# Gate rows transposed on VectorE before they are written, and the linear attention's output products grouped by tile shape

## The chip, the cores and the metric

One program on one core of a Trainium2 chip. Its engines run separate instruction streams and meet at semaphores: TensorE (PE in the profile; PEld is its weight load), VectorE (DVE), ScalarE (ACT), GpSimd (POOL) and SyncE (SP, which here only issues DMAs). Each engine works its stream off in order. Sixteen DMA engines move data between DRAM, the on-chip SBUF and back. The metric is the device time of one execution in microseconds; three executions of the kernel before took 1444.01, 1446.22 and 1446.49, the median is 1446.22.

## The reference: what is computed

Two layers of an encoder trunk over 512 tokens of width 1024, all in f32. A conditioning vector c gives six vectors of 1024 per layer: shift, scale and gate for each of two sub-layers.

```
for l in range(DEPTH):                                   # DEPTH = 2
    mod = silu(c) @ ada_w[l] + ada_b[l]
    sh1, sc1, g1, sh2, sc2, g2 = split(mod, 6)
    hn = rmsnorm(x, pre_mix_g[l]) * (1 + sc1) + sh1
    y = token_mixer(hn, ...)        # retention | stick-breaking | gated linear attention
    x = x + g1 * rmsnorm(y, post_mix_g[l])
    hn = rmsnorm(x, pre_ffn_g[l]) * (1 + sc2) + sh2
    y = conv_ffn(hn, ...)
    x = x + g2 * rmsnorm(y, post_ffn_g[l])
```

The gated linear attention (four heads of 64) works in eight chunks of 64 tokens. A chunk's output is the sum of an inner part, scores of the chunk times its values, and a carried part, the query times the state left by the chunks before:

```
inter = einsum('bhcd,bhde->bhce', q_i * exp(b_i), state)
intra = einsum('bhts,bhse->bhte', scores, v_i)
out_i = inter + intra
```

## The kernel before

Activations lie with the features on the 128 partitions and the 512 tokens along the free dimension, or, for the residual x and for what closes a sub-layer, with the tokens on the partitions in four blocks (`tb` 0 to 3) of 128. A weight product is made of three products of parts (`mm3`, L355): a weight tile `raw` comes by DMA on SP's queue, ScalarE rounds it into `hi` (L351) and VectorE leaves the rest in `lo` (L352). PE's stream is written out by hand-made orders (`TOK` at L55, `PQ` at L53) and a scheduler that keeps each engine's instructions in the order in which it chose them; nothing is reordered on the chip by data arriving late.

**The gates.** `ada_steps` (L238) computes half of one of a layer's six vectors: eight loads of a 128x512 piece of `ada_w` on SP's queue, each multiplied by c on VectorE and summed (L249), then the bias (L254, L255) and, for a gate, the norm's weight (L259). The result is `modT`, 128 partitions by 8 columns, where element (p, k) belongs to feature 128k + p. The calls are spread between other work by `fill`: gate 1 of layer 0 during the first mixer, gate 2 of layer 0 and gate 1 of layer 1 during the first feed-forward part, gate 2 of layer 1 at its very end, while the last products of that part run. A gate must multiply along the free dimension where tokens lie on the partitions (`close0` L503, `close1` L510), so it is turned into a row of 1024 in DRAM (`rows`, L262) and read back to all 128 partitions (`load_gate`, L266). Both DMAs are issued by GpSimd (`QUEUE` sends kind "row" to it). The write at L262 puts each of the 1024 elements to its place separately, as 4 bytes:

```
ld(rows[l, which].rearrange("o (k p) -> p (o k)", p=P), modT[l, which], False, "row")
```

GpSimd also computes every norm's power -1/2 (L285), in order with those DMAs.

**The end of a feed-forward part.** For each token block `close1` squares, multiplies by the gate, loads x (`load_x`, SP's queue), adds (L519), stores x and hands the tile to `prenorm`, whose transposes on PE with the scaled identity `dg` (L303, L321) give the next layer's input. Between them PE already runs the next layer's first projection (`proj_tok`, stick-breaking values, 24 products for a token block into one of three banks `pj`).

**The linear attention's output** (`gla_pair`, L741 to L758) is made for two heads together, in two PSUM banks `o`, one for even and one for odd chunks. For each chunk c in turn two products of 64x64 tiles add the inner part (scores `sc` times values `vtok`) and one product over all 128 rows with 64 columns adds the carried part (states `st` times decayed query `qd`), so tile shapes alternate chunk by chunk. This happens four times: two head pairs in each of two layers. The banks' marks are set anew by `start=True` in each chunk.

Of the kernel before, what the change touches and what calls it, by code (L numbers as in the profile page):

```python
# [11 lines left out]
F32 = mybir.dt.float32  # L12
# [7 lines left out]
P = 128  # L20
S = 512
D = 1024
KT = D // P
# [3 lines left out]
CH = 64  # L27
NCH = S // CH
# [69 lines left out]
def trunk(ctx: ExitStack, tc: tile.TileContext, A, out, dbg=None):  # L98
    nc = tc.nc

    cp = ctx.enter_context(tc.tile_pool(name="cp", bufs=1))
# [15 lines left out]
    def nm(s):  # L117
        cnt[0] += 1
        return f"{s}_{cnt[0]}"

    def T(tag="m", shape=(P, 512), dt=F32):
        tag = TMAP.get(tag, tag)
        return tiles[tag].tile(list(shape), dt, tag=tag, name=nm(tag + "_"))

    def small(n):
        return sp.tile([P, 8], F32, tag="s", name=nm("s"))[:, :n]
# [11 lines left out]
    def pso():  # L138
        return bank("po")
# [4 lines left out]
    V, SC, G, PE = nc.vector, nc.scalar, nc.gpsimd, Recorder(nc.tensor)  # L144

    @contextmanager
    def seq(kind):

        mode = MODE[kind]
        m = (None, PE.last, PE.lastp)[mode]  # L150
        if m is not None:
            with tc.issue_after(m.ins):
                yield
        else:
            yield
        if kind == "p":
            PE.lastp = PE.last

    lastw = [None]
    start = {"on": True, "ld": None, "pe": None, "ws": []}  # L160

    def ld(t, src, gated=False, kind=None):
        q = QUEUE.get(kind, "sp")
        if q != "sp":
            return (G if q == "g" else SC).dma_start(t, src)


        m = lastw[0] if gated else start["ld"]
        if m is None:
            r = nc.sync.dma_start(t, src)  # L170
        else:
            with tc.issue_after(m.ins):
                r = nc.sync.dma_start(t, src)
        if start["on"]:
            start["ld"] = r
        return r
# [57 lines left out]
    modT = {}  # L234
# [3 lines left out]
    def ada_steps(l, g):  # L238
        which, half = WHICH[g // 2], g % 2
        if half == 0:  # L240
            modT[l, which] = cp.tile([P, KT], F32, tag=f"mod{l}{which}", name=f"mod{l}{which}")
        pt = small(8)
        for j in range(4):
            for h in range(2):
                raw = ap_.tile([P, 512], F32, tag="ada", name=nm("ada"))
                r_ = ld(raw, A["ada"][l, g // 2, 4 * half + j, :, 512 * h : 512 * h + 512], False, "ada")
                if "ada" not in QUEUE:
                    lastw[0] = r_
                V.scalar_tensor_tensor(raw, raw, 1.0, cB[h], ALU.mult, ALU.mult, accum_out=pt[:, 4 * h + j : 4 * h + j + 1])  # L249
                if (2 * j + h) % FSTEP == FSTEP - 1:  # L250
                    yield
        m = modT[l, which][:, 4 * half : 4 * half + 4]
        o = PV[which] + 4 * half
        V.tensor_tensor(m, pt[:, 0:4], pt[:, 4:8], ALU.add)  # L254
        V.tensor_tensor(m, m, pv[l][:, o : o + 4], ALU.add)  # L255
        if which[0] == "g":

            o = PV["p" + which] + 4 * half
            V.tensor_tensor(m, m, pv[l][:, o : o + 4], ALU.mult)  # L259
            if half:  # L260
                rows[l, which] = dp.tile([1, D], F32, tag=f"{which}{l}", name=f"{which}row{l}")
                ld(rows[l, which].rearrange("o (k p) -> p (o k)", p=P), modT[l, which], False, "row")  # L262

    rows = {}

# [266 lines left out]
    def mixer(l, hnh, hnl, after):  # L532
# [115 lines left out]
        def gla_pair(j):  # L648
# [14 lines left out]
            sc = T("gl", (P, 2, NCH // 2, CH))  # L663
# [15 lines left out]
            for n in range(len(LEVELS) + 1):  # L679
# [3 lines left out]
                with seq("g"):  # L683
                    for c in range(NCH):
                        odd, cs = 64 * (c % 2), slice(c * CH, c * CH + CH)
# [12 lines left out]
                if n == len(LEVELS):  # L698
                    b3 = b.rearrange("p (c t) -> p c t", t=CH)
                    kd, qd = T("gl"), T("gl")  # L700
# [17 lines left out]
            st = [T("gl", (P, 4, P)) for _ in range(2)]  # L718
# [5 lines left out]
            with seq("g"):  # L724
                for c in range(NCH - 1):
                    rows = slice(64 * (c % 2), 64 * (c % 2) + 64)
                    PE.matmul(pk[c % 2][:, (c // 2) * P : (c // 2) * P + P], kdT[rows, c // 2, :],
                              vtok[c // 2][rows, j * P : j * P + P], start=True, stop=True)
            for c in range(NCH - 1):
                for h in range(2):  # L730
                    rows = slice(64 * h, 64 * h + 64)
# [8 lines left out]

            o = [pso(), (psz, psg)[GB > 0]()]  # L741
            with seq("g"):
                for c in range(NCH):
                    odd = slice(64 * (c % 2), 64 * (c % 2) + 64)
                    cs = slice(c // 2 * CH, c // 2 * CH + CH)
                    for h in range(2):
                        PE.matmul(o[c % 2][64 * h : 64 * h + 64, cs],
                                  vtok[c // 2][odd, j * P + 64 * h : j * P + 64 * h + 64],
                                  sc[odd, h, c // 2, :], start=True, stop=(c == 0), skip_group_check=True)
                    if c:  # L750
                        PE.matmul(o[c % 2][:, cs], st[(c - 1) // 4][:, (c - 1) % 4, :],
                                  qd[:, c * CH : c * CH + CH], start=False, stop=True, skip_group_check=True)
            go[j] = T("gl")
            g4 = go[j].rearrange("p (c o t) -> p c o t", o=2, t=CH)
            for odd in range(2):
# [117 lines left out]
        for u in range(4):  # L873
            wh, wl = unit(A["wo"][l, 0, u], (P, 2, 512))
            for kk in range(2):
                k = KPERM[2 * u + kk]
                for tb in range(NTB):
                    cs = slice(tb * P, tb * P + P)
# [3 lines left out]
        for tb in range(NTB):  # L882
            cs = slice(tb * P, tb * P + P)
            ps = psz()
            for i in range(KT):
                k = KPERM[i]
# [272 lines left out]
```

## Time and profile before

| | |
|---|---|
| median of three executions | 1446.22 us |
| the profiled execution's own time | 1440.25 us |
| its span, first to last instruction | 1438.5 us |
| PE busy | 1374.8 us, 96% of the span |
| DVE busy | 831.9 us, 58% |
| ACT busy | 674.5 us, 47% |
| POOL busy | 36.2 us, 3% |
| mean granted TensorE clock | 0.985 |
| DRAM read, written | 176.51 MB, 8.41 MB |

The profile is one execution; its rows give start and length of each instruction, the idle time before it and what ended that idle time. The profiled execution was 5.97 us shorter than the median of the unprofiled three. A share of busy time is a mean over unlike stages: the two mixers (60 to 345 and 757 to 1045 us in this trace), the two feed-forward parts, the start and the end; what an edit in one of them is worth is read there.

### The profile page before, as it was taken

The page shows a single profiled execution, that of the slowest core. Times are in us where ns is not written, and L with a number is a line of the kernel's source. Part 1 is how long each engine was busy: PE and PEld are TensorE (multiplying, and loading weights), DVE is VectorE, ACT ScalarE, POOL GpSimd, SP SyncE. Part 2 cuts the span into 40 slices and gives each one's busy share as a digit, 9 for nine tenths or more (in the row PEclk, how much of TensorE's full clock was granted, in tenths as well). Part 3 has the DMA queues.
Part 4 walks back from the last instruction along what each step waited for, and adds up shares of the span by engine and source line. Part 5 has one row for each costly group of instructions (what it writes and reads, how often), then busy time and mean ns, then how long its engine had stood idle before and what let it go on. Part 6 is the DMA issues. An engine that isn't in the chain of part 4 may idle for free.

```text
span 1438.5 us, 19727 instructions
## 1 busy us (share of the span) xinstructions
PE 1374.8 (96%) x7619; PEld 1123.4 (78%) x7619; DVE 831.9 (58%) x1544; ACT 674.5 (47%) x1105; POOL 36.2 (3%) x57
## 2 busy tenths in 40 slices
PE   8999789989999999999999999998999999999998
PEld 5887667768878778888879877776789888888886
DVE  4459887655878674432654487586665444443232
ACT  5565466755533233332244676766655333333130
POOL 0000000000000000000010000000010000000000
PEclk9999999999999999999999999999999999999999
DMA  8636461203688762222773221112152222222222
GB/s 312 215 127 151 157 204 51 74 16 134 225 246 264 199 228 95 103 88 103 249 162 127 88 89 59 45 59 74 45 205 101 90 103 90 101 101 90 103 103 103
DMA packets 73614, 186.22 MB, mean 129 GB/s; under 512 B 8448, under 2 KB 9520, under 8 KB 73520
## 3 DMA queue, kind: packets, MB, share of 16 engines
q1 hardware_dynamic: 72512, 182.68, 39.0%
q0 software_dynamic: 704, 2.11, 0.4%
q8 instruction: 60, 0.98, 0.3%
q14 instruction: 34, 0.28, 0.1%
q10 hardware_dynamic: 304, 0.16, 0.0%
HBM read 176.51 MB, written 8.41 MB: 129 GB/s over the span
## 4 chain that ended last, share of the span: by engine, by line
PE 54%; DMA 7%; DVE 7%; ACT 5%; issue 2%; POOL 0%; DVEq 0%; SPq 0%; POOLq 0%; ACTq 0%
PE pj L91 30%; PE ps L91 24%; DMA ada<-ada 6%; DVE lo L352 1%; DVE ada L249 1%; ACT hi L351 1%; DMA m__1230_6531<-x 0%; DMA m__707_3538<-x 0%; DMA raw<-wu 0%; DMA raw<-wT 0%; DVE hnl L332 0%; POOL s L285 0%; ACT m__1645_8747 L577 0%; ACT m__1407_7530 L577 0%; ACT m__1283_6827 L577 0%
## 5 line engine op out<-in xcount | busy, mean ns | idle before, releaser
L352 DVE TENSOR_TENSOR lo<-raw,hi 128x1024 fp32r<-128x1024 f32 (+2 forms) x208 | 245.7, 1184 | 263.3 <-ACT hi L351 258.0
L91 PE MATMUL pj<-hnh,hi 128*128 128x512 f32 x976 | 384.5, 394 | 7.2 <-DVE m__873_4577 L911 3.9
L91 PE MATMUL pj<-hnl,hi 128*128 128x512 f32 x976 | 383.6, 393 | 0.0
L91 PE MATMUL pj<-hnh,lo 128*128 128x512 f32 x976 | 382.7, 392 | 0.0
L351 ACT CAST hi<-raw 128x1024 fp32r<-128x1024 f32 (+2 forms) x208 | 211.1, 1017 | 336.4 <-PE pj L91 177.7
L91 PEld LDWEIGHTS pj<-hnh,hi 128*128 128x128 f32 x976 | 184.5, 189 | 47.6 <-issue 10.2
L91 PEld LDWEIGHTS pj<-hnl,hi 128*128 128x128 f32 x976 | 184.1, 189 | 37.7 <-issue 1.0
L91 PEld LDWEIGHTS pj<-hnh,lo 128*128 128x128 f32 x976 | 184.2, 189 | 37.5
L249 DVE SCALAR_TENSOR_TENSOR ada<-ada,cB 128x512 f32<-128x512 f32 x160 | 107.4, 689 | 45.1 <-DMA ada<-ada 44.5
L91 PE MATMUL pj<-hi,hnh 128*128 128x384 f32 (+1 forms) x160 | 52.8, 330 | 5.1 <-ACT m__1254_6623 L541 3.8
L91 PE MATMUL pj<-lo,hnh 128*128 128x384 f32 (+1 forms) x160 | 52.2, 326 | 0.4 <-DVE lo L352 0.4
L91 PE MATMUL pj<-hi,hnl 128*128 128x384 f32 (+1 forms) x160 | 52.1, 326 | 0.0
L285 POOL TENSOR_TENSOR s<-s,nhalf 128x1 f32<-128x1 f32 x32 | 20.3, 633 | 783.4 <-DVE s L283 779.3
L91 PE MATMUL ps<-hnl,hi 128*128 128x256 f32 x128 | 36.2, 287 | 1.3 <-DVE hnl L332 1.3
L91 PEld LDWEIGHTS pj<-hi,hnh 128*128 128x128 f32 x160 | 31.1, 194 | 6.1 <-ACT m__1254_6623 L541 4.0
L91 PE MATMUL ps<-hnh,lo 128*128 128x256 f32 x128 | 35.8, 283 | 0.0
L91 PE MATMUL ps<-hnh,hi 128*128 128x256 f32 x128 | 35.7, 289 | 0.0
L513 ACT ACTIVATE junk<-ps 128x512 bf16<-128x512 f32 x16 | 9.5, 596 | 52.3 <-PE ps L91 52.0
L91 PEld LDWEIGHTS pj<-lo,hnh 128*128 128x128 f32 x160 | 31.0, 194 | 1.0 <-DVE lo L352 0.7
L91 PEld LDWEIGHTS pj<-hi,hnl 128*128 128x128 f32 x160 | 30.9, 193 | 0.0
L91 PEld LDWEIGHTS ps<-hnl,hi 128*128 128x128 f32 x128 | 24.5, 193 | 1.7 <-DVE hnl L332 1.7
L91 PEld LDWEIGHTS ps<-hnh,hi 128*128 128x128 f32 x128 | 24.6, 197 | 0.0
(2794 smaller groups left out, 2523.5 us busy)
## 6 DMA issues: line engine op xcount, KB each, us to landing
raw<-wu SPq DMA_DIRECT2D x88, 512.0 KB, 3.3
ada<-ada SPq DMA_DIRECT2D x160, 256.0 KB, 3.7
raw<-wd SPq DMA_DIRECT2D x44, 512.0 KB, 3.2
raw<-wT SPq DMA_DIRECT2D x42, 512.0 KB, 3.5
raw<-wo SPq DMA_DIRECT2D x16, 512.0 KB, 3.2
raw<-wsv SPq DMA_DIRECT2D x8, 384.0 KB, 3.5
raw<-wrv SPq DMA_DIRECT2D x8, 384.0 KB, 3.0
raw<-wgv SPq DMA_DIRECT2D x8, 272.0 KB, 2.7
```

The source lines that it names most:

```text
L91: self.last = self.e.matmul(*a, **k)
L249: V.scalar_tensor_tensor(raw, raw, 1.0, cB[h], ALU.mult, ALU.mult, accum_out=pt[:, 4 * h + j : 4 * h + j + 1])
L285: G.tensor_tensor(r, v, nhalf, ALU.pow)
L351: SC.copy(h, raw)
L352: V.tensor_tensor(l_, raw, as32(h), ALU.subtract)
L513: SC.activation(junk, ps, AF.Square, accum_out=ss)
```

## The change

A gate's `modT` is now 128 by 32, with columns 8 to 31 set to zero by GpSimd, and both layers share one buffer for it. VectorE transposes it in 32x32 blocks into `gateT` (one buffer for all gates), after which 32 neighbouring features of the row lie along the free dimension of one partition. Four DMAs on GpSimd's queue, one for each quarter of the partitions, write eight pieces of 128 bytes each. In the linear attention all inner products of a head pair are issued first and all carried ones behind them, and only the first chunk of each bank sets the marks.

```
--- before.py
+++ after.py
@@ -238,7 +238,12 @@
     def ada_steps(l, g):
         which, half = WHICH[g // 2], g % 2
         if half == 0:
-            modT[l, which] = cp.tile([P, KT], F32, tag=f"mod{l}{which}", name=f"mod{l}{which}")
+
+            w = 32 if which[0] == "g" else KT
+            modT[l, which] = cp.tile([P, w], F32, tag=f"mod{which}" if w > KT else f"mod{l}{which}",
+                                     name=f"mod{l}{which}")
+            if w > KT:
+                G.memset(modT[l, which][:, KT:], 0.0)
         pt = small(8)
         for j in range(4):
             for h in range(2):
@@ -259,7 +264,11 @@
             V.tensor_tensor(m, m, pv[l][:, o : o + 4], ALU.mult)
             if half:
                 rows[l, which] = dp.tile([1, D], F32, tag=f"{which}{l}", name=f"{which}row{l}")
-                ld(rows[l, which].rearrange("o (k p) -> p (o k)", p=P), modT[l, which], False, "row")
+                t = cp.tile([P, 32], F32, tag="gateT", name=f"{which}T{l}")
+                V.transpose(t, modT[l, which])
+                r4 = rows[l, which].rearrange("o (k q i) -> q (o k) i", q=4, i=32)
+                for q in range(4):
+                    ld(r4[q], t[32 * q : 32 * q + KT, :], False, "row")
 
     rows = {}
 
@@ -740,16 +749,19 @@
 
             o = [pso(), (psz, psg)[GB > 0]()]
             with seq("g"):
+
+
                 for c in range(NCH):
                     odd = slice(64 * (c % 2), 64 * (c % 2) + 64)
                     cs = slice(c // 2 * CH, c // 2 * CH + CH)
                     for h in range(2):
                         PE.matmul(o[c % 2][64 * h : 64 * h + 64, cs],
                                   vtok[c // 2][odd, j * P + 64 * h : j * P + 64 * h + 64],
-                                  sc[odd, h, c // 2, :], start=True, stop=(c == 0), skip_group_check=True)
-                    if c:
-                        PE.matmul(o[c % 2][:, cs], st[(c - 1) // 4][:, (c - 1) % 4, :],
-                                  qd[:, c * CH : c * CH + CH], start=False, stop=True, skip_group_check=True)
+                                  sc[odd, h, c // 2, :], start=(c < 2), stop=(c == 0), skip_group_check=True)
+                for c in range(1, NCH):
+                    cs = slice(c // 2 * CH, c // 2 * CH + CH)
+                    PE.matmul(o[c % 2][:, cs], st[(c - 1) // 4][:, (c - 1) % 4, :],
+                              qd[:, c * CH : c * CH + CH], start=False, stop=True, skip_group_check=True)
             go[j] = T("gl")
             g4 = go[j].rearrange("p (c o t) -> p c o t", o=2, t=CH)
             for odd in range(2):
```

The order of SP's and ScalarE's instructions is the same as before, apart from line numbers and buffer numbers. On GpSimd's stream the place of layer 1, gate 2 (s are the sums of a norm, nhalf the constant -1/2) reads before:

```order
L285 TENSOR_TENSOR s_6374<-s_6371,nhalf 128x1
L165 DMA g2row_6314<-mod1g_6155 128x8x1
L285 TENSOR_TENSOR s_6392<-s_6389,nhalf 128x1
L285 TENSOR_TENSOR s_6439<-s_6436,nhalf 128x1
L285 TENSOR_TENSOR s_6457<-s_6454,nhalf 128x1
```

and now:

```order
L294 TENSOR_TENSOR s_6398<-s_6395,nhalf 128x1
L165 DMA g2row_6333<-g2T_6334 8x32 x4
L294 TENSOR_TENSOR s_6416<-s_6413,nhalf 128x1
L294 TENSOR_TENSOR s_6463<-s_6460,nhalf 128x1
L294 TENSOR_TENSOR s_6481<-s_6478,nhalf 128x1
```

One DMA has become four at the same place, between the same two norms; nothing else moved there.

On VectorE's stream at the same gate, the addition of the bias, the norm's weight and what follows, before:

```order
L283 TENSOR_SCALAR s_6371<-s_6371 128x1
L255 TENSOR_TENSOR mod1g_6155<-mod1g_6155,pv_658 128x4
L259 TENSOR_TENSOR mod1g_6155<-mod1g_6155,pv_658 128x4
L519 SCALAR_TENSOR_TENSOR m__1201_6376<-m__1108_5962,s_6374,m__1201_6376 128x512
L519 SCALAR_TENSOR_TENSOR m__1202_6377<-m__1198_6369,s_6374,m__1202_6377 128x512
```

and now:

```order
L264 TENSOR_TENSOR mod1g_6173<-mod1g_6173,pv_658 128x4
L268 STREAM_TRANSPOSE g2T_6334<-mod1g_6173 128x32
L528 SCALAR_TENSOR_TENSOR m__1201_6400<-m__1108_5980,s_6398,m__1201_6400 128x512
L528 SCALAR_TENSOR_TENSOR m__1202_6401<-m__1198_6393,s_6398,m__1202_6401 128x512
L291 TENSOR_TENSOR s_6413<-s_6409,s_6410 128x1
L292 TENSOR_SCALAR s_6413<-s_6413 128x1
```

The transpose stands directly behind the gate's last operation and ahead of the two additions to x of token block 1.

On TensorE's stream the output of layer 0, head pair 1 (m__450 are the scores, m__154 to m__160 the values of the four token blocks, m__570 the decayed query, m__574 and m__575 the states), before, in its first ten rows:

```order
L91 MATMUL ps_3016<-m__450_2300,m__154_783 64x64 x2
L91 MATMUL ps_3017<-m__450_2300,m__154_783 64x64 x2
L91 MATMUL ps_3017<-m__570_2905,m__574_2943 128x64
L91 MATMUL ps_3016<-m__450_2300,m__156_810 64x64 x2
L91 MATMUL ps_3016<-m__570_2905,m__574_2943 128x64
L91 MATMUL ps_3017<-m__450_2300,m__156_810 64x64 x2
L91 MATMUL ps_3017<-m__570_2905,m__574_2943 128x64
L91 MATMUL ps_3016<-m__450_2300,m__158_837 64x64 x2
L91 MATMUL ps_3016<-m__570_2905,m__574_2943 128x64
L91 MATMUL ps_3017<-m__450_2300,m__158_837 64x64 x2
```

and now, in its first twelve:

```order
L91 MATMUL ps_3022<-m__450_2306,m__154_783 64x64 x2
L91 MATMUL ps_3023<-m__450_2306,m__154_783 64x64 x2
L91 MATMUL ps_3022<-m__450_2306,m__156_810 64x64 x2
L91 MATMUL ps_3023<-m__450_2306,m__156_810 64x64 x2
L91 MATMUL ps_3022<-m__450_2306,m__158_837 64x64 x2
L91 MATMUL ps_3023<-m__450_2306,m__158_837 64x64 x2
L91 MATMUL ps_3022<-m__450_2306,m__160_864 64x64 x2
L91 MATMUL ps_3023<-m__450_2306,m__160_864 64x64 x2
L91 MATMUL ps_3023<-m__570_2911,m__574_2949 128x64
L91 MATMUL ps_3022<-m__570_2911,m__574_2949 128x64
L91 MATMUL ps_3023<-m__570_2911,m__574_2949 128x64
L91 MATMUL ps_3022<-m__570_2911,m__574_2949 128x64
```

The seven 128x64 products, which stood one by one between 64x64 groups, stand together behind the eight groups. In the whole program the 28 products of this kind form 28 separate runs before and 6 now, not counting other products of the full array that fall among them.

## Rows read from the trace of the kernel before

**Rows 1.** The page of the whole span, its part 1: busy time of each engine (us), share of the span, number of instructions.

```profile
PE 1374.8 (96%) x7619; PEld 1123.4 (78%) x7619; DVE 831.9 (58%) x1544; ACT 674.5 (47%) x1105; POOL 36.2 (3%) x57
```

**Rows 2.** The list of DMA issues: destination<-source, queue, operation, count, size, and last the median us from issue to landing. The first three are gate rows that GpSimd writes (the landing of the fourth is not resolved); the last two are loads of the residual x, the first of them 1.9 us after the fourth gate row was issued, the second 18 us after it.

```profile
g1row<-mod0g POOLq DMA_DIRECT2D x1, 4.0 KB, 10.0
...
g2row<-mod0g POOLq DMA_DIRECT2D x1, 4.0 KB, 9.8
...
g1row<-mod1g POOLq DMA_DIRECT2D x1, 4.0 KB, 11.4
...
m__1213_6441<-x SPq DMA_DIRECT2D x1, 256.0 KB, 11.3
...
m__1229_6530<-x SPq DMA_DIRECT2D x1, 256.0 KB, 4.1
```

**Rows 3.** The DMA rate of the stretch 399 to 413 us in 40 equal slices of 0.35 us, GB/s. The gate row of layer 0, gate 2, is issued at 401.14 us, in the seventh slice.

```profile
GB/s 316 287 228 181 304 351 380 357 375 304 322 281 281 285 262 237 241 152 70 47 35 12 59 47 23 23 64 35 41 35 35 88 23 64 29 135 146 140 111 334
```

**Rows 4.** The timelines of POOL, DVE and PE around layer 1, gate 2: start us, us, engine, line, operation, out<-in, shapes, count, and in brackets the idle time before it and what ended it. m__1213 is the residual tile of token block 2; dg is the scaled identity of its norm; the PE rows from 745.44 are the 24 products of the stick-breaking values for token block 0, those from 756.39 the 24 for token block 1.

```profile
730.34 0.93 POOL L165 DMA_DIRECT2D g2row<-mod1g  x1
...
743.64 0.75 DVE L519 SCALAR_TENSOR_TENSOR m__1213_6441<-m__1110_5966,s,m__1213_6441 128x512 f32<-128x512 f32 x1 [6.50 <-DMA m__1213_6441<-x]
...
745.44 0.42 PE L91 MATMUL pj<-hi,hnh 128*128 128x384 f32 x1
...
748.38 0.44 PE L91 MATMUL pj<-lo,hnh 128*128 128x384 f32 x1 [0.41 <-DVE lo L352]
...
750.42 1.05 PE L91 MATMUL pj<-dg,m__1213_6441 128*128 128x128 f32 x8
...
756.39 0.69 PE L91 MATMUL pj<-hi,hnh 128*128 128x384 f32 x1 [3.85 <-ACT m__1254_6623 L541]
...
763.52 1.05 PE L91 MATMUL pj<-dg,m__1229_6530 128*128 128x128 f32 x8
```

**Rows 5.** The same timelines at the three gates before that: DVE and PE at layer 0, gate 1 (rows from 147 to 158 us), at layer 0, gate 2 (411 to 418) and at layer 1, gate 1 (497 to 510). Between 413.47 and 417.87 PE starts 12 products, between 506.32 and 510.04 nine.

```profile
147.60 0.69 DVE L249 SCALAR_TENSOR_TENSOR ada<-ada,cB 128x512 f32<-128x512 f32 x1 [3.50 <-DMA ada<-ada]
...
149.75 0.69 DVE L386 SCALAR_TENSOR_TENSOR m__279_1479<-pj,m__277_1477 64x512 fp32r<-64x512 f32 x1 [1.45 <-ACT m__277_1477 L385]
...
153.72 1.13 PE L91 MATMUL ps<-m__284_1511,m__283_1510 64*64 64x64 f32 x32 [7.25 <-DVE m__284_1511 L674]
...
158.15 0.53 PE L91 MATMUL pj<-hnh,hi 128*128 128x512 f32 x1
...
411.17 0.69 DVE L249 SCALAR_TENSOR_TENSOR ada<-ada,cB 128x512 f32<-128x512 f32 x1 [5.35 <-DMA ada<-ada]
...
413.47 0.47 PE L91 MATMUL pj<-hnh,hi 128*128 128x512 f32 x1 [3.28 <-DVE m__762_3927 L911]
...
417.87 0.39 PE L91 MATMUL pj<-hnh,hi 128*128 128x512 f32 x1
418.10 0.40 PE L91 MATMUL pj<-hnl,hi 128*128 128x512 f32 x1
...
497.67 0.69 DVE L249 SCALAR_TENSOR_TENSOR ada<-ada,cB 128x512 f32<-128x512 f32 x1 [2.75 <-DMA ada<-ada]
...
506.32 0.52 PE L91 MATMUL pj<-hnh,hi 128*128 128x512 f32 x1 [3.92 <-DVE m__873_4577 L911]
...
510.04 0.40 PE L91 MATMUL pj<-hnh,hi 128*128 128x512 f32 x1
```

**Rows 6.** Stretches: from:to us, length, busy us (and instructions) of PE, PEld, DVE, ACT and POOL, granted TensorE clock, DMA share, GB/s. The first follows the wait of layer 0, gate 1, the second that of layer 1, gate 2.

```profile
154.00:165.00 11.00, 11.00 (x108) 8.40 (x104) 10.34 (x27) 3.77 (x6) 0.98 (x2) 0.80 0.17 58
...
756.00:759.00 3.00, 2.61 (x8) 2.61 (x9) 2.27 (x7) 2.36 (x6) 0.55 (x1) 0.50 0.71 232
```

**Rows 7.** The timeline of PE: two 64x64 groups with a 128x64 product between them, out of the linear attention's output of layer 0, pair 1 (303 us); a block of 32 tiled products of a score level with the instruction behind it (870 us); four 128x128 transposes with the instruction behind them (1002 us).

```profile
303.78 0.33 PE L91 MATMUL ps<-m__450_2300,m__156_810 64*64 64x64 f32 x4
304.04 0.43 PE L91 MATMUL ps<-m__570_2905,m__574_2943 128*128 128x64 f32 x2
304.41 0.33 PE L91 MATMUL ps<-m__450_2300,m__156_810 64*64 64x64 f32 x4
...
870.14 0.69 PE L91 MATMUL ps<-m__1425_7623,m__1424_7622 64*64 64x64 f32 x32
870.77 0.50 PE L91 MATMUL pj<-hnh,hi 128*128 128x512 f32 x1
...
1002.70 0.66 PE L94 MATMUL ps<-ident,m__1667_8904 128*128 128x128 f32 x4
1003.11 0.47 PE L91 MATMUL ps<-m__1646_8755,m__1570_8373 128*128 128x512 f32 x1
```

**Rows 8.** The timeline of SP's queue: the one other small write to DRAM in the trace, c's row in eight pieces of 512 bytes (38.74 us), and the load that reads it back and must wait for it (43.37 us).

```profile
38.74 0.37 SPq L173 DMA_DIRECT2D crow<-m__1_93  x1
...
43.37 0.80 SPq L173 DMA_DIRECT2D cB<-crow  x2
```

**Rows 9.** Timelines of DVE and POOL around layer 1, gate 2: a DVE operation over 128x128, the DVE operation that follows the gate's last one, and POOL's next instruction after the gate row's issue.

```profile
725.80 0.29 DVE L303 TENSOR_SCALAR dg<-ident,s 128x128 f32<-128x128 f32 x1 [0.43 <-POOL s L285]
...
730.43 0.75 DVE L519 SCALAR_TENSOR_TENSOR m__1201_6376<-m__1108_5962,s,m__1201_6376 128x512 f32<-128x512 f32 x1 [0.38 <-POOL s L285]
...
733.29 0.56 POOL L285 TENSOR_TENSOR s<-s,nhalf 128x1 f32<-128x1 f32 x1 [2.01 <-DVE s L283]
```

## The prediction

> **What bounds the kernel now.** I read the page first: TensorE is busy 96% of the span [rows 1], so anything that removes idle time of PE, or shortens what PE must do, can move the end, and little else can. Then I looked for what the change touches and who waits there.
>
> The list of DMA issues shows something odd about the gate rows: 4 KB each, yet they land 9.8 to 11.4 us after their issue, and a load of x issued 1.9 us after the fourth of them needs 11.3 us where the same load needs 4.1 us a little later [rows 2]. The DMA strip shows why: some 4 us after the row's issue the rate of all 16 engines falls from around 300 GB/s to between 12 and 88 GB/s and stays there for 18 slices, 6.3 us [rows 3]. The 1024 pieces, 64 for each engine, pass at 6.3/64 = 0.10 us a piece, 0.16 us if the whole landing time is theirs, and everything queued behind them waits.
>
> Who pays is read in the timelines. At layer 1, gate 2, the row goes out at 730.34; VectorE sits 6.50 us for the x tile of block 2, and behind it in their orders stand the casts of weights on ScalarE and the copy that frees the bank for the next projection; PE waits 0.41 and 3.85 us [rows 4]. At the three gates before, VectorE waits for `ada` pieces (3.50, 5.35 and 2.75 us), and PE then waits for VectorE: 7.25 us at 153.72, 3.28 at 413.47, 3.92 at 506.32 [rows 5].
>
> After each of these waits the granted clock is at its lower level, 1.2 instead of 2.4 GHz (0.50 in the whole stretch 756 to 759 [rows 6]), so the wait costs more than its length. Of the 24 products from 756.39 to 763.52, 7.13 us, the like 24 of block 0 took 4.98 us with a wait of 0.41 inside [rows 4]: 7.13 - 4.57 = 2.56 us lost. Twelve products from 413.47 took 4.40 us where the rate a moment later is 0.23 each: 1.64 lost; nine from 506.32 took 3.72: 1.65 lost; at 153.72 half of 4.43 us: 2.2 [rows 5].
>
> The second half of the change concerns PE alone. In the linear attention's output a 64x64 group and a 128x64 product together take 0.63 us from one group to the next (303.78 to 304.41), though 32 tiled products in a row need 0.63 us, 0.08 for four, and a 128x128 transpose 0.10 [rows 7].
>
> **The change, part by part.**
>
> *Gate rows.* The 4 x 1024 pieces of 4 bytes become 4 x 32 of 128 bytes. At 0.10 to 0.16 us a piece, 32 pieces occupy one engine for 5.0 us if all fall on one, 0.3 us if they spread over sixteen; each transfer has eight pieces from eight partitions, so I take them as spread over several engines and the hold as under 1 us. The nearest row is c's own row, eight pieces of 512 bytes: its reader starts 4.6 us after its issue, in the thick of other loads [rows 8].
>
> With the hold gone:
> - Layer 1, gate 2: x for block 2 lands near 736.5 (issue plus the 4.1 us of the undisturbed load), some 7 us earlier; all of VectorE's and ScalarE's work behind it moves into time in which they stand idle, and PE's order there has no other wait that is as late. Gain 3.85 + 0.41 + 2.56 = 6.8 us.
> - Layer 0, gate 2: 3.28 + 1.64 = 4.9. Layer 1, gate 1: 3.92 + 1.65 = 5.6. Both lie in the feed-forward part, where PE otherwise does not wait.
> - Layer 0, gate 1: 7.25 + 2.2 would be 9.4, but behind it VectorE is busy 10.34 of 11 us [rows 6] and sets the pace itself. What it gets back is its own idle time, 3.50 + 1.45 [rows 5], so 5.0.
>
> Sum 22.3 us; if at the first three only half is found, 14.6; if the first gives all, 26.7.
>
> *What is added.* Four transposes on VectorE. No row shows one; the nearest are 0.29 us for an operation over 128x128 [rows 9] and, below, nothing. At layer 1, gate 2, VectorE idles 0.38 us just there, waiting for GpSimd [rows 9], so it is covered; at the others it is at most 0.3 us each behind waits that are gone. I take 0; without cover 1.2 us in all. VectorE's queue behind a transpose holds the x additions, so a late operand would count; its operands are VectorE's own results and columns that GpSimd cleared 80 us or more earlier, or at the start. The one buffer `gateT` is read by DMAs of the gate before, 83 us earlier at the least.
>
> The Trainium skill's page "VectorE: DVE Perf Modes" (The three transpose paths) gives 311 ns for a 128x128 bf16 transpose on VectorE; as an estimate from it, four such would make 1.2 us and leave the sum as it is.
>
> GpSimd issues four DMAs for one. An issue takes 0.93 us now [rows 4]; four at no more than that end by 734.1, while the next norm on GpSimd starts at 733.29 [rows 9]: at worst 0.8 us late, and its `dg` is needed by PE only some 10 us later. Nothing. The four clearing operations stand on GpSimd far from any norm. The broadcast load behind each row may start earlier than now, but the layer-1 ones wait for the gate buffer anyway.
>
> *Grouping.* Of 28 runs of 128x64 products 6 remain; 22 alternations go. Each costs 0.63 us now; in a group the 64x64 four cost 0.08 and a 128x64 product, two passes, between 0.10 and 0.21 (one or two transposes' worth) [rows 7]; with up to twice 0.08 where the same tiles follow one another. So 22 x (0.25 to 0.44) = 5.5 to 9.7 us less PE time, 7.6 in the middle. In both mixers PE has little idle time and the two second pairs lie directly on the way to the output projection; beside the first pair of layer 0 VectorE is the busier one. I take 85%: 6.5 us.
>
> Together 22.3 + 6.5 = 28.8 us: the profiled execution's 1440.25 would become 1411.5. That execution was 5.97 us under the median; taken from the median, 1446.22 - 28.8 = 1417 us.
>
> **Rivals.**
> 1. *Short pieces stay dear.* 128 bytes cost more than 4 bytes did, or gather on few engines; the hold is 5 us, half of now. Against it: c's row. Half the gates' gain, 11 + 6.5: 1429 us. Chance 0.14. The Trainium skill's page "DMA: Bandwidth & Descriptors" (Specifications) speaks for this one: full rate needs pieces of at least 512 bytes, and shorter ones are read, modified and written. No row here separates that from the plain count of pieces.
> 2. *The next late thing.* With the hold gone, the usual wait for `ada` or for VectorE's backlog keeps half of each wait at the first three gates. For: VectorE is nearly full there [rows 6]. 14.6 + 6.5 = 21.1: 1425 us. Chance 0.14.
> 3. *Grouping is worth nothing*, because each PE product there waits for its operands anyway: 1424 us. Chance 0.07. Against: no waits stand in the rows at 303 us.
> 4. *More than the sum*: the first gate gives all 9.4 and the grouping 9.7: 1410 us. Chance 0.05.
> 5. *It doesn't do what it says*: the slump of the DMA engines was not the pieces' doing. Grouping alone then leaves 1440 us; chance 0.05, and within 0.2% of 1446 in more than half of that, if grouping fails too. Against: all landings that are resolved show it, each at a gate row.
> 6. *Slower*: the price belongs to the transfer, not to its pieces. Four transfers of 10 us hold the engines 40 us. At layer 1, gate 2, x for block 2 would land 30 us later, with nothing for PE to do: 1446.22 + 30 - 6.5 = 1470 us or more. It decides from about 17 us for the four together. Against: c's row again, one transfer, under 4.6 us. Chance 0.02, and 0.01 for anything else on that side.
>
> **How the numbers follow.** The forecast, 1417 us, has 0.52. Rivals 1 to 3 end at 1424 to 1429, rival 4 at 1410; with some 3 us of spread between executions, 1408 to 1432 holds them all and leaves rivals 5 and 6 out, under 0.1, and the tails. A difference of 0.2%, 2.9 us, is about what a measurement of this kernel tells from none. Faster by more 0.94, within 0.03, slower 0.03.
>
> **What would show it.** Right: the four gate rows land in under 4 us, the rate beside them stays above 100 GB/s, PE's waits of 7.25, 3.28, 3.92 and 3.85 us are gone or under 1.5 us and the lower clock behind them too, and the linear attention's output of a pair takes about 2.5 us instead of 4.3. Wrong: x loads behind layer 1, gate 2 still landing in 8 us or more (rivals 1, 6), PE waits of 2 us or more at the same places with another releaser (rival 2), or new PE waits of the same length behind the grouped products (rival 3).

## The result, and the profile after

The changed kernel takes **1412.10 us** (median of four executions, 1409.92 to 1415.45) against 1446.36 for the kernel before; the ratio is 0.977, 95% interval 0.9755 to 0.9786, that is 31 to 35 us less. The forecast was 1417. Its profiled execution took 1413.02 us, 27.2 less than the profiled execution of before, which lay 6 us under its median; so the two traces show 27 of the 34 us.

The page, part 1 (as [rows 1]), and the list of DMA issues (as [rows 2]), of the kernel after:

```profile
PE 1364.1 (97%) x7619; PEld 1115.6 (79%) x7619; DVE 832.1 (59%) x1548; ACT 675.1 (48%) x1105; POOL 41.3 (3%) x73
```

```profile
m__1213_6465<-x SPq DMA_DIRECT2D x1, 256.0 KB, 3.6
...
g1row<-g1T POOLq DMA_DIRECT2D x8, 1.0 KB, 4.2
g2row<-g2T POOLq DMA_DIRECT2D x8, 1.0 KB, 3.4
```

The gate rows land in 3.4 to 4.2 us (medians) instead of 9.8 to 11.4, and the x tile behind the last gate in 3.6 instead of 11.3. The DMA rate around layer 0, gate 2 (394 to 408 us, 40 slices, as [rows 3]; the row is issued at 396.15, in the seventh slice) is under 100 GB/s for two slices, 0.7 us, where before it was for 17, 6.0 us:

```profile
GB/s 252 375 328 345 287 246 293 299 228 257 257 277 259 264 287 324 353 319 328 305 222 117 0 35 187 386 374 398 316 328 281 246 187 252 339 392 398 386 386 281
```

PE at the four gates, the instructions that answer to those of [rows 4] and [rows 5] (start, us, engine, line, operation, in brackets the idle time ahead):

```profile
147.01 0.69 PE L91 MATMUL ps<-m__284_1512,m__283_1511 64*64 64x64 f32 x32 [1.00 <-DVE m__284_1512 L683]
...
401.71 0.39 PE L91 MATMUL pj<-hnh,hi 128*128 128x512 f32 x1
...
404.43 0.39 PE L91 MATMUL pj<-hnh,hi 128*128 128x512 f32 x1
...
478.78 0.47 PE L91 MATMUL pj<-hnh,hi 128*128 128x512 f32 x1 [0.71 <-DVE m__857_4504 L923]
...
489.77 0.39 PE L91 MATMUL pj<-hnh,hi 128*128 128x512 f32 x1
...
491.81 0.39 PE L91 MATMUL pj<-hnh,hi 128*128 128x512 f32 x1
...
727.20 0.42 PE L91 MATMUL pj<-hi,hnh 128*128 128x384 f32 x1
...
733.17 0.42 PE L91 MATMUL pj<-hi,hnh 128*128 128x384 f32 x1
...
737.07 0.33 PE L91 MATMUL pj<-lo,hnh 128*128 128x384 f32 x1
```

The waits of 7.25, 3.28, 3.92 and 3.85 us are down to 1.00 and nothing. The product that began at 413.47 and that at 417.87 now begin at 401.71 and 404.43: 2.72 us apart instead of 4.40, so the lower clock behind the wait is gone too.

Since PE's order hardly changed, its instructions can be paired one by one over the whole program; how much earlier the later kernel starts each of them tells where the time comes from:

| place (time in before) | lead ahead of it | lead behind it | gained | forecast |
|---|---|---|---|---|
| layer 0, gate 1 (130.06 to 158.52) | -0.30 | 8.62 | 8.9 | 5.0 |
| linear attention, layer 0, pair 0 (196.84 to 206.50) | 6.35 | 7.54 | 1.2 | |
| all from 158.52 to 303.14, that pair included | 8.62 | 6.03 | -2.6 | |
| linear attention, layer 0, pair 1 (303.14 to 307.42) | 6.03 | 8.10 | 2.1 | |
| layer 0, gate 2 (409.12 to 417.87) | 8.32 | 13.44 | 5.1 | 4.9 |
| layer 1, gate 1 (491.13 to 510.04) | 13.45 | 18.23 | 4.8 | 5.6 |
| layer 1, gate 2 (745.44 to 763.16) | 18.24 | 26.09 | 7.9 | 6.8 |
| linear attention, layer 1, pair 0 (904.22 to 911.77) | 26.15 | 27.56 | 1.4 | |
| linear attention, layer 1, pair 1 (1005.59 to 1009.96) | 27.10 | 27.39 | 0.3 | |
| the last product | | 27.24 | | |

Of the 8.9 at the first gate 2.6 are given back before 303 us, 3.8 if the 1.2 of the pair's grouping are left out. Two stretches of the kernel after, and then the stretches of the kernel before that hold about the same work (columns as in [rows 6]), show where most of it goes: the granted clock is lower in the kernel after, 0.68 instead of 0.79 and 0.83 instead of 1.00. Why it is lower there isn't shown.

```profile
184.00:200.00 16.00, 14.33 (x88) 12.21 (x88) 14.17 (x33) 9.83 (x18) 0.00 (x0) 0.68 0.76 237
210.00:220.00 10.00, 9.53 (x39) 6.79 (x40) 5.26 (x8) 6.39 (x13) 0.00 (x0) 0.83 0.01 2
```

```profile
192.00:208.00 16.00, 14.07 (x87) 11.39 (x86) 13.54 (x33) 10.27 (x19) 0.00 (x0) 0.79 0.68 227
216.00:226.00 10.00, 9.00 (x46) 6.90 (x46) 5.21 (x8) 7.84 (x16) 0.00 (x0) 1.00 0.04 14
```

The block of layer 0, pair 1, as in [rows 7]: eight 64x64 groups in 0.63 us, seven 128x64 products in 1.58, together 2.21 us from 297.11 to the next instruction at 299.32, where before it was 303.14 to 307.42, 4.28 us.

```profile
297.11 0.34 PE L91 MATMUL ps<-m__450_2306,m__154_783 64*64 64x64 f32 x8
...
297.74 1.10 PE L91 MATMUL ps<-m__570_2911,m__574_2949 128*128 128x64 f32 x8
298.68 0.83 PE L91 MATMUL ps<-m__570_2911,m__575_2950 128*128 128x64 f32 x6
299.32 0.48 PE L91 MATMUL ps<-m__558_2845,m__477_2435 128*128 128x512 f32 x1
```

At layer 1, pair 1, the same grouping gained 0.3 us only: the last states come from VectorE, whose chain of 12 state operations (L746), six for each head and each needing its head's one before, runs from 979.18 to 982.90, as long as before (1006.27 to 1009.99), and PE waits 0.28 us for it (PE's row, then VectorE's):

```profile
981.79 0.97 PE L91 MATMUL ps<-m__1668_8929,m__1676_8958 128*128 128x64 f32 x4 [0.28 <-DVE m__1676_8958 L746]
```

```profile
979.18 1.84 DVE L746 SCALAR_TENSOR_TENSOR m__1675_8957<-m__1675_8957,s,ps 64x64 f32<-64x64 f32 x6
981.05 0.59 DVE L746 SCALAR_TENSOR_TENSOR m__1676_8958<-m__1675_8957,s,ps 64x64 f32<-64x64 f32 x2
981.68 1.22 DVE L746 SCALAR_TENSOR_TENSOR m__1676_8958<-m__1676_8958,s,ps 64x64 f32<-64x64 f32 x4
```

### The profile page after: what moved, and what is told of

It is laid out like the page before. It is cut to its first block, busy times and chain, and to the rows that moved or that the text cites. A ratio compares the mean times of both kernels' runs of the same rounds, so it can differ in the third digit from the quotient of the medians.

```text
span 1411.2 us, 19759 instructions
## 1 busy us (share of the span) xinstructions
PE 1364.1 (97%) x7619; PEld 1115.6 (79%) x7619; DVE 832.1 (59%) x1548; ACT 675.1 (48%) x1105; POOL 41.3 (3%) x73
## 4 chain that ended last, share of the span: by engine, by line
PE 55%; DVE 7%; DMA 6%; ACT 5%; issue 2%; POOL 0%; DVEq 0%; POOLq 0%; ACTq 0%; SPq 0%
PE pj L91 31%; PE ps L91 24%; DMA ada<-ada 5%; DVE ada L254 1%; DVE lo L361 1%; ACT hi L360 1%; DMA m__707_3544<-x 0%; DMA m__1783_9428<-x 0%; DMA raw<-wu 0%; DMA raw<-wT 0%; DVE hnl L341 0%; ACT m__1407_7554 L586 0%; ACT m__1283_6851 L586 0%; ACT m__1645_8771 L586 0%; ACT m__1468_7842 L586 0%
```

## The experiments

Ratios are to the kernel before on the same chip, with 95% intervals; the kernel before took 1450 to 1451 us there.

### Each half alone

The gate rows of the change on the kernel before:

> The gate-row half alone, linear attention as before. Theory (the 1024 four-byte pieces hold the DMA engines, and the waits behind them go): the four gates give 22 to 26 us, so a ratio of 0.982 to 0.985 to the kernel before. Rival (the gate rows give what was forecast, 22 us at most, and the surplus of the measured 33 us comes from the grouping): the ratio is 0.985 or above, and the grouping alone must then show 10 us or more.

Measured: 1422.09 us, ratio 0.9809 (0.9783 to 0.9835), some 28 us less. The grouping alone:

> The grouping alone, gate rows as before. Theory (each alternation of tile shape costs PE 0.25 to 0.44 us, and some of it is given back to VectorE): 5 to 7 us, a ratio of 0.995 to 0.9965. Rival (the grouping carries the surplus): 10 to 11 us, 0.9925. Rival (PE waits for its operands there anyway): within 0.1% of 1.

Measured: 1442.91 us, ratio 0.9950 (0.9928 to 0.9971), 7.3 us less. The two multiply to 0.976, and the whole change has 0.977: the parts add up, and most of the surplus over the forecast lies in the gate rows.

### Fewer pieces without the transpose

```
-ld(rows[l, which].rearrange("o (k p) -> p (o k)", p=P), modT[l, which], False, "row")
+ld(rows[l, which].rearrange("o (p k) -> p (o k)", k=KT), modT[l, which], False, "row")
```

> The kernel before with one thing changed: each gate row is written in 128 pieces of 32 bytes, in one transfer (element 128k + p lands at 8p + k, so the gate's features are permuted and the output is not the reference's). No transpose, no clearing, no further transfers; every engine's order is that of before. Theory (the price is the number of pieces, 0.10 us each on sixteen engines): the hold falls from 6.3 to 0.8 us and the time is that of the gate-row half alone within 0.2%, ratio 0.982 to 0.985. Rival (the price belongs to a scattered write as such, or to pieces far below 128 bytes): the landing stays at 8 us or more and the ratio above 0.993. If what the changed kernel adds (transposes, clearing, three more transfers per gate) costs anything, this one is faster than the gate-row half alone by that.

Measured: 1422.67 us, ratio 0.9805 (0.9779 to 0.9830), the same as the gate-row half. So all that the gate rows gain is in how the row is written, and what the change adds (transposes, clearing, three more transfers a gate) costs nothing that can be measured. A transpose takes 0.21 us:

```profile
711.62 0.21 DVE L268 STREAM_TRANSPOSE g2T<-mod1g 128x32 f32<-128x32 f32 x1
```

### The scattered write added to the changed kernel

```
+extra = dp.tile([1, D], F32, tag=f"{which}{l}s", name=f"{which}scat{l}")
+ld(extra.rearrange("o (k p) -> p (o k)", p=P), modT[l, which][:, :KT], False, "row")
```

> The changed kernel, and behind the four transfers of each gate a fifth one that writes the same 1024 elements in four-byte pieces to a second row that nobody reads. The gate itself is as early as in the changed kernel. Theory (what costs is that the pieces hold the engines, and other loads queue behind them): the waits of PE at the four gates come back, 20 to 26 us, 1432 to 1438 us, ratio to the kernel before 0.990 to 0.995. Rival (what costs is that the gate's own row arrives late): nothing comes back, ratio 0.977.

Measured: 1443.73 us, ratio 0.9953 (0.9938 to 0.9969), what the grouping has alone. PE's waits at the four gates are back:

```profile
155.06 1.14 PE L91 MATMUL ps<-m__284_1512,m__283_1511 64*64 64x64 f32 x32 [7.45 <-DVE m__284_1512 L685]
...
413.93 0.77 PE L91 MATMUL pj<-hnh,hi 128*128 128x512 f32 x1 [5.10 <-DVE m__762_3936 L925]
...
510.31 0.77 PE L91 MATMUL pj<-hnh,hi 128*128 128x512 f32 x1 [6.57 <-DVE m__873_4593 L925]
...
762.27 0.69 PE L91 MATMUL pj<-hi,hnh 128*128 128x384 f32 x1 [3.48 <-ACT m__1254_6655 L552]
```

The experiment tells less than it was meant to: the scattered write was issued ahead of the four transfers, so the gate's own row landed late as well (11.4 and 11.6 us). The next one separates the two by accident.

### 640 pieces instead of 1024

```
+ld(rows[l, which][:, :512].rearrange("o (k p) -> p (o k)", p=P), modT[l, which][:, :4], False, "row")
+ld(rows[l, which][:, 512:].rearrange("o (p k) -> p (o k)", p=P), modT[l, which][:, 4:8], False, "row")
```

> The kernel before, with the first half of each gate row written as before (512 pieces of 4 bytes) and the second half in 128 pieces of 16 bytes (in permuted order, so those gate elements are not the reference's): 640 pieces instead of 1024, in two transfers. Theory (0.10 us a piece, sixteen engines): the hold falls from 6.3 to 4 us, each of PE's four waits by about 2.4 us, the slower clock behind them stays: 9 to 12 us less, ratio 0.992 to 0.9935. Rival (the queues take up a short hold, and only the last microseconds of a long one cost): 15 us or more, ratio under 0.990. Rival (any scattered write has a fixed price): ratio 1 or above, since there are now two.

Measured: 1445.76 us, ratio 0.9959 (0.9941 to 0.9977): 6 us less, no theory's number. The trace shows why. The first half of a gate is ready some 20 us before the second, so its 512 pieces went out at 117.14 instead of 133, and there they held the loads of `ada`: VectorE waits 6.27 us, then PE 6.29 (VectorE's row, then PE's). At the old place of this gate the wait is gone, though the gate's row was complete no sooner than before.

```profile
130.39 0.69 DVE L249 SCALAR_TENSOR_TENSOR ada<-ada,cB 128x512 f32<-128x512 f32 x1 [6.27 <-DMA ada<-ada]
```

```profile
132.40 0.47 PE L91 MATMUL ps<-m__256_1333,tri 128*128 128x128 f32 x1 [6.29 <-ACT m__256_1333 L778]
```

At the other gates the four-byte pieces go out earlier too, but PE's wait doesn't always move with them. At layer 0, gate 2, they go out at 389.28; VectorE waits for `ada` at once, and PE pays 20 us later, at the same product as before, 6.44 us instead of 3.28 (VectorE's row, then PE's):

```profile
400.23 0.69 DVE L249 SCALAR_TENSOR_TENSOR ada<-ada,cB 128x512 f32<-128x512 f32 x1 [4.50 <-DMA ada<-ada]
```

```profile
420.50 0.77 PE L91 MATMUL pj<-hnh,hi 128*128 128x512 f32 x1 [6.44 <-DVE m__762_3928 L912]
```

The loads that are held are those behind the four-byte pieces, not those around the time at which the row is needed; PE can pay for it later. The second halves, 128 pieces of 16 bytes, land in 1.8 to 4.3 us. But half of the pieces cost nearly all of it, which the count of pieces doesn't explain.

### The scattered write twice

The same two lines as in the fourth kernel, added to the kernel before.

> The kernel before with every scattered write done twice, the second time to a row that nobody reads: 2048 pieces of 4 bytes at each gate. Theory (pieces add up): the hold grows by 6.3 us, and nothing is left to hide it: 25 us more, 20 to 30 with the clock, ratio 1.014 to 1.021. Rival (the price is a fixed latency of a scattered write, and two overlap): 1.000 to 1.004.

Measured: 1461.76 us, ratio 1.0083 (1.0056 to 1.0109), 12 us more, half of what the count of pieces asks, and more than the rival allows. At the first gate the second write lands only a little behind the first (12.8 us from an issue 1.1 us later, against 10.4), at the last one far behind it (18.9 us from an issue 0.9 us later, against 12.2), and there x for block 2 lands in 18.8 us, where before it took 11.3:

```profile
g1row<-mod0g POOLq DMA_DIRECT2D x1, 4.0 KB, 10.4
g1scat<-mod0g POOLq DMA_DIRECT2D x1, 4.0 KB, 12.8
...
m__1213_6449<-x SPq DMA_DIRECT2D x1, 256.0 KB, 18.8
...
g2scat<-mod1g POOLq DMA_DIRECT2D x1, 4.0 KB, 18.9
```

At the four gates the second write lands 3.4, 3.1, 0.9 and 7.6 us behind the first. The last of these is a little more than the 6.3 us that the count of pieces asks, the third hardly a price at all; why they differ isn't shown.

### The price of a write by itself

> The changed kernel with twelve writes added that nobody reads, one or two at a time, some 22 us apart, in the second layer's first half of the feed-forward part, where the loads of weights land in 3.3 us and use a fifth of the DMA engines' time. Read is the time from issue to landing of each. In this order: 1024 pieces of 4 bytes (as in a gate row before); 512 of 4 (128 partitions, 4 each); 256 of 4; 128 of 4; two writes of 1024 of 4 at once; 128 of 32 bytes; 1024 of 8; 1024 of 32; 512 of 4 from 64 partitions; 1024 of 4 on SP's queue; 1024 of 64. Theory (the price goes by pieces, about 0.1 us each on sixteen engines, whatever their size): 2 to 3 us of latency plus 6.3 us for 1024 pieces of 4, 8 or 32 bytes alike (8 to 10 us), 5 to 6 for 512, 4 for 256, 3 for 128 of either size, 14 to 16 for the second of the two. Rival (the price goes by size, four-byte pieces being a case of their own): 1024 pieces of 32 bytes land in 4 us or less, and 128 to 512 pieces of 4 as slowly as 1024. Rival (the hold comes of GpSimd's queue): on SP's queue the landing is 4 us or less.

Measured in one execution, from issue to landing (the list of DMA issues; a name gives a letter and the count, the letters going in the order of issue, pa to pl, that the expectation lists; pk, on SP's queue, isn't resolved):

```profile
pl1024x<-m__2060_11296 POOLq DMA_DIRECT2D x1, 64.0 KB, 4.4
...
pi1024x<-m__1994_10858 POOLq DMA_DIRECT2D x1, 32.0 KB, 4.4
...
pa1024x<-m__1840_9834 POOLq DMA_DIRECT2D x1, 4.0 KB, 9.9
...
pb512x<-m__1862_9980 POOLq DMA_DIRECT2D x1, 2.0 KB, 11.7
...
pc256x<-m__1884_10126 POOLq DMA_DIRECT2D x1, 1.0 KB, 9.4
pd128x<-m__1906_10272 POOLq DMA_DIRECT2D x1, 0.5 KB, 8.1
pe1024x<-m__1928_10418 POOLq DMA_DIRECT2D x1, 4.0 KB, 11.7
pf1024x<-m__1928_10418 POOLq DMA_DIRECT2D x1, 4.0 KB, 11.6
pg128x<-m__1950_10566 POOLq DMA_DIRECT2D x1, 4.0 KB, 1.7
ph1024x<-m__1972_10712 POOLq DMA_DIRECT2D x1, 8.0 KB, 5.6
pj512x<-m__2016_11004 POOLq DMA_DIRECT2D x1, 2.0 KB, 10.8
```

The theory of the count falls for 128 to 1024 pieces. 128 pieces of four bytes, half a KB in all, land in 8.1 us, 1024 of them in 9.9, two times 1024 in 11.7 and 11.6; 1024 pieces of eight bytes need 5.6, of 32 and of 64 bytes 4.4, and 128 of 32 bytes 1.7. Pieces of four bytes are a case of their own. Even the 128 of them hold the engines for 14 slices: the DMA rate from 1135 to 1155 us, 40 slices of 0.5 us, with the write issued at 1138.39, in the seventh (the gaps at either side are pauses in the loading):

```profile
GB/s 262 303 49 0 0 0 0 0 33 116 197 270 131 33 33 49 25 0 33 0 49 49 49 49 49 16 8 197 410 287 49 0 0 0 0 0 156 238 442 213
```

It isn't GpSimd's queue either: behind the write on SP's queue, two loads of weights have a median landing of 11.3 us, where 3.2 to 3.3 is usual there.

The same run shows the other half of the matter. PE's instructions in this stretch keep their distance: against another profile of the changed kernel, this run is 1.86 us behind at 1050 us, ahead of all twelve writes, and 1.86 at the end. Eight slow writes cost PE nothing where loads run far enough ahead, and four cost 28 us where they do not.

### How the saving of the grouping comes about

```
 for c in range(NCH):
     ... inner products of chunk c ...
+    if c % 2:
+        for e in (c - 1, c):
+            if e:
+                carried(e)
```

> The changed kernel, with the linear attention's products grouped chunk pair by chunk pair (inner of two chunks, then carried of the two) instead of all inner first; the marks are set as in the changed kernel. Read at layer 0, pair 1, where the block stands undisturbed on PE: 4.28 us before (seven runs of 128x64 products), 2.21 us changed (one run). Theory (every alternation costs the same): four runs, so 2.21 + 3 x 0.345 = 3.25 us. Rival (the saving is due to the marks being set once, not to the order): 2.2 us.

Measured in one execution: the block takes 3.10 us (299.36 to 302.46), so it is the order, 0.30 us for each of three runs more, where whole grouping saved 2.07 us for six, 0.345 each.

```profile
299.36 0.34 PE L91 MATMUL ps<-m__450_2306,m__154_783 64*64 64x64 f32 x8
...
302.46 0.48 PE L91 MATMUL ps<-m__558_2845,m__477_2435 128*128 128x512 f32 x1
```

### Further: no change of tile shape, and half of the states' chain

The states of two heads are kept as 128x64 and moved on by one VectorE operation; the carried products become 64x64 tiles too. They go into a bank of their own, which VectorE adds at the end.

```
+V.scalar_tensor_tensor(st[:, c, :], st[:, c - 1, :], dl[:, c : c + 1], src, ALU.mult, ALU.add)
...
+PE.matmul(oc[rows, (c - 1) * CH : c * CH], st[rows, c - 1, :], qd[rows, c * CH : c * CH + CH],
+          start=(c == 1), stop=True, skip_group_check=True)
...
+V.tensor_tensor(go[j][:, CH:], go[j][:, CH:], oc[:, : 7 * CH], ALU.add)
```

> The changed kernel, taken further: the carried products of the linear attention are made of 64x64 tiles as well, into a bank of their own that VectorE adds at the end, and the states are kept as 128x64, so that one VectorE operation moves both heads' state on. No alternation of tile shape is left inside the block, VectorE has 7 operations for 14 in a state's chain and one addition of 128x448 more. Theory (alternations and VectorE's state chain are what bounds these blocks): 0.5 us less at each of three pairs, 1 to 2 us less at the last pair of layer 1, where PE waits for the chain: 2 to 4 us, 1408 to 1410 us against 1412, ratio to before 0.974 to 0.976. Rival (PE isn't on the path there any more, or the bank taken is missing elsewhere): 0.977 or above.

Measured: 1408.12 us, ratio 0.9702 (0.9679 to 0.9724). Since that is more than expected, both kernels ran once more side by side:

> The changed kernel once more, beside the next two on one chip: ratio to the kernel before 0.975 to 0.979.

> The version with all products of the linear attention's output in 64x64 tiles, once more, beside the changed kernel on the same chip. If its gain is real (its states' chain on VectorE is half as long and no alternation is left): 3 to 6 us under the changed kernel, ratio 0.970 to 0.974. If the two earlier ratios differed by chip and chance: within 2 us of it.

Measured: 1415.58 us, 0.9758 (0.9738 to 0.9778), for the changed kernel; **1405.30 us, 0.9686 (0.9665 to 0.9707)**, for this one: 10 us less, more than the 3 to 6 expected, and the fastest version here. The block of layer 0, pair 1, takes 1.44 us (294.90 to 296.34) instead of 2.21; the rest is not taken apart. Most of it shows in the second mixer, where the scheduler also put other instructions into another order: a wait of PE for the linear attention's decays (L683) is down from 4.63 to 1.42 us, and the lower clock that followed it is gone (1.00 where the changed kernel has 0.50 and 0.62; two rows of the changed kernel's second run from the wait's end on, then one of this version).

```profile
970.00:973.00 3.00, 3.00 (x38) 1.65 (x40) 2.99 (x6) 1.58 (x3) 0.00 (x0) 0.50 0.34 96
973.00:976.00 3.00, 3.00 (x19) 1.54 (x16) 0.56 (x1) 0.45 (x1) 0.00 (x0) 0.62 0.21 85
```

```profile
963.00:966.00 3.00, 2.90 (x48) 1.65 (x48) 2.99 (x6) 1.70 (x4) 0.00 (x0) 1.00 0.29 86
```

### A row without a transpose, read in steps

```
-V.tensor_tensor(y, ps, g[:, 0:512], ALU.mult)
+V.tensor_tensor(y.rearrange("q (k p) -> q k p", p=P), ps.rearrange("q (k p) -> q k p", p=P),
+                g.rearrange("q (p k) -> q k p", k=KT)[:, 0:4, :], ALU.mult)
```

> The version with 64x64 tiles, and the gate row written without any transpose: one transfer of 128 pieces of 32 bytes into a row in the order 8p + k, loaded as it stands, and the multiplication by the gate at each sub-layer's end reads it with a step of 8 elements. The result is the reference's. Theory (transposes, clearing and three of the four transfers cost nothing where they stand, and a stepped operand costs VectorE nothing): within 2 us of the version with transposes. Rival (stepped reads are slower on VectorE, by 0.3 us and more in each of the 32 multiplications, of which those behind the last products lie on the path): 3 us slower or more.

Measured: 1409.46 us, ratio 0.9730 (0.9706 to 0.9754), 4 us slower than the version with transposes, but the intervals touch, so the loss of the whole program isn't clear of noise. For the operation itself the rival holds: the multiplication reads with a step of 8 and takes 1.12 us instead of 0.69 (the same instruction in this version and in the one before), and PE's waits for `dg` in the projection rise from 3.4 to 6.1 us in sum.

```profile
L517 DVE TENSOR_TENSOR m__659_3353<-ps,g x1: 1123/1123/1123, 333.0 to 333.0; 128x512 f32<-128x512 f32 x1
```

```profile
L524 DVE TENSOR_TENSOR m__659_3359<-ps,g x1: 692/692/692, 332.8 to 332.8; 128x512 f32<-128x512 f32 x1
```

The Trainium skill's page "SBUF — State Buffer" (Door 1: The DMA port swizzle) says that accesses which go to a new 16-byte line each time pay a penalty; the step here is 32 bytes, and the row agrees in direction. In VectorE's time the transposes are the better bargain: four times 0.21 us against 32 times 0.43.

## Why the prediction was right, point by point

- **The place of the loss: right.** While the row writes land, the DMA engines' rate is down, loads queue behind them, VectorE and then PE wait, and the clock falls behind each wait. The waits went with the writes, came back with them, and at the first gate moved with them when half of a write moved.
- **The price, "0.10 us a piece": wrong in kind.** The step divided a slump of 6.3 us by 64 pieces an engine (the strip of [rows 3] has 17 slices under 100 GB/s, 6.0 us, not 18). The separate writes show a price that hardly goes by the count up to 1024: 8.1 us for 128 pieces of four bytes, 9.9 for 1024; a second 1024 added 0.9 to 7.6 us. The gain was read from the waits and needed only a hold of under 1 us, and that came because the change leaves four-byte pieces for 128-byte ones. It makes the pieces fewer and larger at once; the step credited the number, the size was what counted, and that the two went together was luck. By the same row of writes eight bytes, 5.6 us for 1024, would probably have shortened the hold already. Half the pieces, on which the step counted for 9 to 12 us, bring 6 us.
- **Rival 1, short pieces stay dear: no.** 128-byte rows land in 3.4 to 4.2 us. The Trainium skill's page "DMA: Bandwidth & Descriptors" (Specifications) puts the line for the full rate at 512 bytes. That line doesn't decide here: 32-byte pieces land in 1.7 us and four-byte ones in 8.1, both far below it.
- **The term of the gates, 22.3 us: right in the traces, too small for the medians.** By the table the gates gave 8.9, 5.1, 4.8 and 7.9 us at their places, and 3.8 of the first were lost again, so 22.9 stay. The first gate kept 5.1 for the 5.0 forecast, but not in the way that was said: VectorE, busy 10.88 of the 11 us from 148 us on, didn't hold PE back there, and the loss came later, with the clock. Layer 1, gate 2, gave 7.9 for 6.8; the other two 5.1 and 4.8 for 4.9 and 5.6, the last less a new wait of 0.71 us. From trace to trace the whole change saved 27.2 us for 28.8 forecast. Between the medians the gate rows alone saved 28 us (23.9 to 31.5). The forecast took waits read in one execution, 6 us under its median, from the median, and that execution showed the waits at their mild end: with the same writes the kernel with the grouping alone, profiled in an execution of 1443.75 us near its median, waits 8.64 us at the first gate and 4.05 at the second, where [rows 5] have 7.25 and 3.28. That this makes up the whole difference isn't shown.

```profile
155.17 1.13 PE L91 MATMUL ps<-m__284_1511,m__283_1510 64*64 64x64 f32 x32 [8.64 <-DVE m__284_1511 L674]
...
413.46 0.47 PE L91 MATMUL pj<-hnh,hi 128*128 128x512 f32 x1 [4.05 <-DVE m__762_3927 L912]
```

- **Rival 2, the next late thing keeps half: no** at two of its three gates. At the first, 3.8 of 8.9 us were lost again, though with the lower clock and not at the same place; with the gate rows alone, with transposes and without, it was 2.2 of 8.9 and 1.1 of 7.7.
- **Rivals 3 and 5: no.** Grouping alone gave 7.3 us, and the gate rows alone 28.
- **Rival 4, more than the sum:** its number, 1410 us, lies nearer to the 1412.10 measured than the forecast does, but not for its reasons: the first gate kept 5.1 us and not 9.4, the grouping gave 7.3 and not 9.7.
- **What is added costs nothing: right** (the third experiment).
- **The grouping, 6.5 us: right in sum, 7.3 (4.2 to 10.4), not in its parts.** An alternation costs 0.30 to 0.345 us, inside the 0.25 to 0.44 of the prediction. "The two second pairs lie directly on the way" holds for layer 0, 2.1 us; at layer 1 VectorE's chain of states sets the end, and 0.3 us remain. The table has 1.2, 2.1, 1.4 and 0.3 us at the four pairs, where the clock plays a part too.
- **Rival 6, a transfer has the price: no.** Four transfers land in 3.4 to 4.2 us (medians), if not all under the 4 us named, and the rate beside the four of layer 0, gate 2, is under 100 GB/s for 0.7 us only.

## What to carry to other kernels

A transfer of a few KB can bring the rate of all DMA engines down; look at the DMA rate for slumps and at what lands late behind them, and count elements that are written one by one. Whether a slump costs anything is decided by how far the loads around it run ahead: move such a write to a stretch with slack, or make its pieces larger; 32 bytes were enough here. Where products of different tile shapes alternate, group them by shape, and then look which engine feeds the last of them.

## What the runs showed of the hardware

Single writes of four-byte pieces to DRAM took 8.1 to 12.3 us over all runs whether there were 128 or 1024 of them, from GpSimd's queue, and the DMA rate stayed between 0 and 49 GB/s meanwhile (the strip of the 128); a second write of 1024 beside a first took 11.5 to 18.9 us. With eight bytes to a piece 1024 of them took 5.6 us. Why four bytes are a case of their own was not found, nor whether the engines or the DRAM hold the loads up; in these runs neighbouring pieces also lie side by side in DRAM and come from different partitions, and pieces of four bytes far apart were not tried. A step of 8 elements in one operand made a VectorE multiplication over 128x512 take 1.12 us instead of 0.69.
